# Other ticks for squares and scalings in a hybrid decoder block, all FFN quarter sums on VectorE, and the last four banks emptied by ScalarE

## The chip, the cores and the metric

The kernel runs on one core of a Trainium2 chip. The metric is the time of one execution on the device in microseconds (us); lower is better. Several engines work side by side, each through its own instructions in order, and wait for each other by semaphores: TensorE (PE, matmuls and transposes), VectorE (DVE), ScalarE (ACT), GpSimd (POOL) and SyncE (SP), whose queue issues nearly all DMA transfers. Matmul results lie in PSUM banks, which have to be read by VectorE or ScalarE before PE may write them anew.

## The reference

One decoder block over 1024 tokens of width 1024, in float32. What matters here, cut from the reference:

```python
h = rms_norm(x, g_pre_mix)
z = h @ w_in                                  # q, k, v of 24 heads, GLU input, two gates
q, k, v, glu_in, z_ga, z_gc = jnp.split(z, ...)
y_attn = dilated_attention_mixer(q, k, v, ...)
y_conv = conformer_conv_mixer(glu_in, ...)    # u * sigmoid(gate), causal conv, layer norm, silu
merged = sigmoid(z_ga) * y_attn + sigmoid(z_gc) * y_conv
x = x + rms_norm(merged @ w_mix_out, g_post_mix)
h = rms_norm(x, g_pre_ffn)
gate, up = jnp.split(h @ w_ffn_in, 2, axis=-1)
x = x + rms_norm((silu(gate) * up) @ w_ffn_out, g_post_ffn)
```

## The kernel before

Nearly all large products run as float16 matmuls of 128x512. Each operand is split into a high part (a cast, or a scaled copy, on ScalarE) and a low part (the remainder, on VectorE or POOL), and three matmuls make one product: high by high, high by low, low by high. Such a group of three is a *tick*, the unit in which the program plans: `B.later(n, step)` writes a step into the program n ticks later, and `tick()`, called behind each group of three, emits the steps that are due and moves the background generators on (`yield n` in one lets n ticks pass). There is no other scheduler. The order of each engine's instructions is the order in which the steps are emitted, and each engine waits at its next instruction until its inputs and its buffer are there.

Products that come in twos (two 128-column weight blocks against both halves of the tokens: the GLU with its gate, the second gate, q and k, and the FFN's two inputs) run as a *Winograd pair*, `winograd`: seven products in place of eight, A11, A12, S2, S1, S3, S4, A22, four ticks each, 28 ticks in all, in two banks X and Z (then V). Between them ScalarE copies a bank out: x1 after A11 (L552), x2 after S2 (L557), v1 after S1 (L562). S2 needs the first copy done, S3 the second and S4 the third, since they write on in the bank; A22 needs X read by the callback f22, which is L991 in a GLU pair and L2047 in an FFN pair. f11, f22, f12 and f21 put the results together.

For each pair the weights are prepared during the pair before. `load_ahead` issues the loads (L343 is their line), `peaks` squares them on ScalarE with a running sum (L135; the name in the trace is `junk<-d` or `junk<-b`), which bounds their size, `scales` makes powers of two of it with a small matmul on PE (L151, its input `pb` from L142), `prescale` scales whole blocks on ScalarE (L204) where the weights are used in several sums, and `quarters` makes the weight combinations: step 3 the sums for S3 and S4 (L403, L404), step 4 their split (L376, or L367 where the scale goes along; the low part is L377 on POOL or L368 on VectorE), step 5 that of A22. `pair` plans these by ticks: prescale at PRE and PRE + 1, step 4 at tick 8.

On the other side stand the token combinations: T1, T2 and then T3, T4 by `quarter_sums`, a generator, from the normed tokens. `split` makes cast (L1448) and low part (L1449).

The stages, in order: norm of x; plain GLU products and the first Winograd pair of the GLU (from about 115 us); the GLU, gate, and q/k pairs (to about 550 us); v and attention; the mix-out product (L1843) tile by tile of 128 tokens, each tile followed by `mix_norm`: residual, norm (L1563, L1565 on ScalarE), and for the fourth tile of each half, `tt == 3` and `tt == 7`, 8 groups of four transposes (L1573) into two banks with the tag "s", each emptied by ScalarE (L1579) and split. Before a tile is normed, all earlier norms but the last are run to their end (`B.finish`). Then the FFN: two plain steps (`ffn_half`, L526 the last line of their matmuls), 20 Winograd pairs, and the output product (L2170) as a Winograd product of the whole, seven products of 11 steps by four banks.

In the FFN pairs the results of two pairs are put into sums and written out to memory (`sums`, `spill`, L1899: names dqA11, dqS3 and so on), and the squares of these results (`measure`, L1872) and of the output weights (`w_square`, L1877, load L1876, name w_fo) are taken for a common scale. The loads of w_fo stand in SP's queue behind the writes of the pair before.

In the output product (`splits` is its operand work: L367 on ScalarE, L368 on VectorE, a row of 11 steps at a time) the four banks X are added at the end of product 5 into the rows `C[1]` (L2200 on VectorE), and product 6 goes on in the same banks. `right1` then squares (L2105) and scales (L2148) these rows.

Of the kernel before, what the change touches and what calls it, by code (L numbers as in the profile page):

```python
# [21 lines left out]
H = 512  # L22
# [15 lines left out]

PC = (18, 20, 26)

LF, PK, SC, PRE = 14, 22, 2, 5

TINY, W_TOP, H_TOP, A_TOP = 2.0 ** -60, 2.0 ** -13, 256.0, 2.0 ** -13

# [8 lines left out]
PLAIN = 2  # L53
# [18 lines left out]
class Build:  # L72
# [48 lines left out]

        self.nc.vector.tensor_scalar(dst.bitcast(I32), src.bitcast(I32), 0x7F800000, None, op0=OP.bitwise_and)

    def peaks(self, i):

        nc = self.nc
        m = self.tiny(2, "pk", 4)
        kind = self.jobs[i][2]
        raws = [self.raw[i - 1], self.raw[i]] if kind in ("row2", "second") else [self.raw[i]]
        for c, r in enumerate(raws):  # L130
            q = self.junk
# [3 lines left out]
            nc.scalar.activation(q, r, AF.Square, scale=W_TOP, accum_out=m[:, c:c + 1])  # L135
        q = None
        self.peak[i] = self.total(m, len(raws))

    def total(self, m, n):
        p = self.tiny(1, "pb", 4, BF16)  # L140
# [314 lines left out]
        self.flush(i)  # L455
        return self.hl.pop(i)

    def ready(self, jobs, load, peaks, scales, parts):

        i = jobs[-1]  # L460
        if load is not None:
            self.later(load, lambda: self.load_ahead(i))
        if i not in self.f16:
            self.later(parts[0], lambda: self.queue_split(i))
            return
        self.planned.update(jobs)
        if i not in self.early:
            self.later(peaks, lambda: self.peaks(i))
# [19 lines left out]
    def pair(self, i):  # L488


        J = self.jobs
        self.load_ahead(i)
        self.queue_split(i)
        self.flush(i)
        n, t = i + 1, self.ticks
        todo = [(1, lambda: self.quarters(i, 3)), (8, lambda: self.quarters(i, 4)), (10, lambda: self.quarters(i, 5))]
        if n < len(J) and J[n][2] == "row1":
            if n + 2 < len(J) and J[n + 2][2] == "row1":
                todo += [(LF, lambda: self.load_ahead(n + 3)), (PK, lambda: self.peaks(n + 3))]
# [12 lines left out]
        return self.hl[i]  # L512
# [64 lines left out]
            rest()  # L577
        f21(X)

    def quarter_sums(self, B, blocks, dt=F32R, by=None):  # L580
# [6 lines left out]
        def keep(name, x, by=None):  # L587
            x = self.split(x, H, dt, None, by)
            T[name].append((x[:, :H], x[:, H:]))


        for i in range(4):
            b11, b12, b22 = B[0][i], B[1][i], B[1][i + 4]
            t1 = self.half()
            nc.vector.tensor_tensor(t1, b11, b12, op=OP.subtract)
            nc.vector.scalar_tensor_tensor(b11, t1, -1.0, b22, op0=OP.mult, op1=OP.subtract)
            keep("T1", t1)
            yield 1
            keep("T2", b11)
            yield 3  # L600
        self.T = T
        for i in range(4):
            b11, b12, b21, b22 = B[0][i], B[1][i], B[0][i + 4], B[1][i + 4]
            if by:
                by.tensor_tensor(b22, b22, b12, op=OP.subtract)
                nc.vector.scalar_tensor_tensor(b21, b11, -1.0, b21, op0=OP.mult, op1=OP.subtract)
                yield 1
                keep("T4", b21)
                yield 0
                keep("T3", b22, by)  # L610
                yield 0
                continue
            self.wsplit.tensor_tensor(b22, b22, b12, op=OP.subtract)
            nc.vector.scalar_tensor_tensor(b21, b11, -1.0, b21, op0=OP.mult, op1=OP.subtract)
            yield 0
            keep("T3", b22)
            yield 1
            keep("T4", b21)
            yield 0
# [819 lines left out]
        x, self.spare = self.spare, None  # L1439
        return x  # L1440

    def split(self, src, n, dt=F32R, w=None, by=None):
# [5 lines left out]
        nc.scalar.copy(s[:, :n], src)  # L1448
        (by or nc.vector).tensor_tensor(s[:, 512:512 + n], src, f(s[:, :n]), op=OP.subtract)  # L1449
        return s  # L1450

    def rhs(self, ops):
# [102 lines left out]
    def mix_norm(self, tt, banks, x):  # L1555
# [9 lines left out]
        nc.scalar.activation(hn, x2, AF.Copy, scale=r)  # L1565
        self.hn[tt // 4].append(hn)
        if tt % 4 == 3:
            yield 8
            op, y = [], None
            for kt in range(8):  # L1570
                ps = self.bank("s")
                for i in range(4):
                    nc.tensor.transpose(ps[:, i * 128:(i + 1) * 128], self.hn[tt // 4][i][:, kt * 128:(kt + 1) * 128], self.ident)  # L1573
# [5 lines left out]
                nc.scalar.activation(y, ps, AF.Copy, scale=self.gain[1][:, kt:kt + 1])  # L1579
# [12 lines left out]
def build(ctx, tc, aps):  # L1592
# [81 lines left out]
    conv = B.conv()  # L1674
    next(conv)
    i = glu_pairs[0]
    B.ready((i - 1, i), 2, 14, 24, (26, 27, 31, 34, 40))
    B.later(22, lambda: B.load_ahead(i + 2))
    B.later(37, lambda: B.peaks(i + 2))
    for j in range(3, FIRST):  # L1680
# [190 lines left out]
    def measure(n, x):  # L1871
        nc.scalar.activation(B.junk[:, :H], x, AF.Square, scale=W_TOP, accum_out=sq[:, n:n + 1])  # L1872

    def w_square(n):
        x = B.slot()
        nc.sync.dma_start(x, aps["w_fo"][n])  # L1876
        B.later(14, lambda: nc.scalar.activation(B.junk, x, AF.Square, scale=W_TOP, accum_out=sw[:, n:n + 1]))  # L1877

    def power_of(dst, inv, cols):
        nc.vector.tensor_reduce(dst, cols, AX.X, OP.max)  # L1880
# [40 lines left out]
    def ffn_half(j, hf, W):  # L1921
        o = B.half()
        ps = B.unit(W[0], B.rhs(B.h2[hf]), KT)
        nc.scalar.activation(o, ps, AF.Silu, scale=B.scale[fi[j][0]][1])
        ps = B.unit(W[1], B.rhs(B.h2[hf]), KT)
        nc.vector.scalar_tensor_tensor(o, ps, B.scale[fi[j][1]][1], o, op0=OP.mult, op1=OP.mult)
        held[j, hf] = o

    B.wsplit = nc.vector
    Ws, i = [], fi[PLAIN][1]  # L1930
    B.ready((i - 1, i), 1, 12, 22, (24, 26, 30))
    B.later(46, lambda: B.load_ahead(i + 2))
# [15 lines left out]
    for j in range(0, PLAIN, 2):  # L1948
# [12 lines left out]
        x = None  # L1961

        for n in range(3):
            B.later(30 + 5 * n + j, lambda n=n, f=plain_sums: f(n))
# [71 lines left out]
    for j in range(PLAIN, FT):  # L2036
# [39 lines left out]
        if j > PLAIN:  # L2076
            for c, x in enumerate(done):
                B.later(1 + c, lambda c=c, x=x, n=2 * j - 1: measure(n + c, x))
            done = x = None
            for c in range(1 + (j < 8)):  # L2080
                if w_sent < FT:
                    B.later(1 + 4 * c, lambda n=w_sent: w_square(n))
                    w_sent += 1
        if j == FT - 2:
            assert w_sent == FT
# [35 lines left out]
            yield gap  # L2121
        C[h][t] = X2[h * 4 + t] = None

    X2, bg = {}, []

    def x2_load(i):
        X2[i] = B.slot()
# [32 lines left out]
    for i in range(7):  # L2160
# [35 lines left out]
        elif i == 5:  # L2196
            for t in range(4):
                x2_load(4 + t)
                c = C[1][t][:, R]
                nc.vector.tensor_tensor(c, X[t], c, op=OP.add)  # L2200
            bg.append(B.bg(right1()))

    for t in range(4):
# [83 lines left out]
```

## Time and profile before

| what | us |
|---|---|
| runs of the kernel: median, lowest, highest | 1616.94, 1616.76, 1619.1 |
| the profiled execution, whole | 1617.35 |
| its span in the trace | 1615.5 |
| PE busy in it | 1584.3 |
| VectorE, ScalarE, POOL busy | 1255.6, 1061.6, 460.5 |

PE's clock is granted in full (0.999 on average). In the lists of waits each row names who waited (engine, tile, line), for whom, the total in us, how often, and the longest. A timeline row gives start, duration, engine, line, operation, output and input names without their numbers, shapes, and in brackets the idle time just before it and who ended it. Rows of the windows give start and end, length, and for each engine busy time and count of instructions. `d` and `b` are weight or token blocks in SBUF, `c` half-width blocks, `p` PSUM banks.

### The profile page before, as it was taken

The page shows a single profiled execution, that of the slowest core. Times are in us where ns is not written, and L with a number is a line of the kernel's source. Part 1 is how long each engine was busy: PE and PEld are TensorE (multiplying, and loading weights), DVE is VectorE, ACT ScalarE, POOL GpSimd, SP SyncE. Part 2 cuts the span into 40 slices and gives each one's busy share as a digit, 9 for nine tenths or more (in the row PEclk, how much of TensorE's full clock was granted, in tenths as well). Part 3 has the DMA queues.
Part 4 walks back from the last instruction along what each step waited for, and adds up shares of the span by engine and source line. Part 5 has one row for each costly group of instructions (what it writes and reads, how often), then busy time and mean ns, then how long its engine had stood idle before and what let it go on. Part 6 is the DMA issues. An engine that isn't in the chain of part 4 may idle for free.

```text
span 1615.5 us, 25559 instructions
## 1 busy us (share of the span) xinstructions
PE 1584.3 (98%) x9052; PEld 897.6 (56%) x9052; DVE 1255.6 (78%) x2426; ACT 1061.6 (66%) x2024; POOL 460.5 (29%) x380
## 2 busy tenths in 40 slices
PE   8999999999999999999999999899999999999997
PEld 6744444444444799976657876444444444444443
DVE  6889999988899768787686655866666666777887
ACT  6476666778786568877752566667666666465654
POOL 0006777767777343654401200200000000000000
PEclk9999999999999999999999999999999999999999
DMA  4353333456665765677847432054344333494424
GB/s 175 109 201 112 112 131 144 146 181 206 198 179 134 234 189 159 173 226 226 249 156 274 179 118 91 27 182 163 138 144 157 124 124 137 148 382 135 156 92 163
DMA packets 162075, 265.56 MB, mean 164 GB/s; under 512 B 63665, under 2 KB 82796, under 8 KB 161948
## 3 DMA queue, kind: packets, MB, share of 16 engines
q1 hardware_dynamic: 157740, 251.77, 47.0%
q0 software_dynamic: 3920, 11.91, 2.3%
q8 instruction: 71, 1.16, 0.3%
q14 instruction: 56, 0.46, 0.1%
q10 hardware_dynamic: 288, 0.27, 0.0%
HBM read 190.05 MB, written 78.55 MB: 166 GB/s over the span
## 4 chain that ended last, share of the span: by engine, by line
PE 77%; DVE 11%; ACT 5%; issue 3%; POOL 2%; DMA 2%; SPq 0%; DVEq 0%; ACTq 0%; POOLq 0%
PE p L538 12%; PE p L540 12%; PE p L539 12%; PE p L2170 10%; PE p L522 4%; PE p L526 4%; PE p L524 4%; PE p L1843 3%; PE p L1188 2%; PE p L1190 2%; PE p L1192 2%; DVE p L931 2%; PE p L785 2%; PE p L1320 2%; PE p L1283 2%
## 5 line engine op out<-in xcount | busy, mean ns | idle before, releaser
L538 PE MATMUL p<-b,b 128*128 128x512 f16 x1032 | 390.9, 379 | 5.8 <-ACT c L552 3.6
L540 PE MATMUL p<-b,b 128*128 128x512 f16 x1032 | 391.1, 379 | 1.5 <-POOL b L377 1.5
L539 PE MATMUL p<-b,b 128*128 128x512 f16 x1032 | 391.0, 379 | 0.0
L2170 PE MATMUL p<-b 128*128 128x512 f16 x924 | 199.8, 379 | 1.1 <-DVE b L2200 1.1
L540 PEld LDWEIGHTS <-b 128*128 128x128 f16 x1032 | 100.9, 98 | 125.2 <-POOL b L377 4.0
L539 PEld LDWEIGHTS <-b 128*128 128x128 f16 x1032 | 100.8, 98 | 123.1 <-issue 7.5
L538 PEld LDWEIGHTS <-b 128*128 128x128 f16 x1032 | 100.9, 98 | 121.0
L931 DVE SCALAR_TENSOR_TENSOR p<-b,par,p 128x511 f32<-128x511 f32 (+14 forms) x232 | 163.9, 738 | 0.0
L2170 PEld LDWEIGHTS <-b 128*128 128x128 f16 x924 | 90.3, 98 | 110.3 <-issue 1.5
L522 PE MATMUL p<-b,b 128*128 128x512 f16 (+1 forms) x368 | 141.3, 384 | 1.6 <-ACT b L367 1.6
L526 PE MATMUL p<-b,b 128*128 128x512 f16 (+1 forms) x368 | 140.7, 382 | 0.4 <-DVE b L368 0.4
L524 PE MATMUL p<-b,b 128*128 128x512 f16 (+1 forms) x368 | 140.6, 382 | 0.0
L368 DVE SCALAR_TENSOR_TENSOR b<-d,sc,b 128x1024 f16<-128x1024 f32 x40 | 51.3, 1281 | 86.1 <-ACT b L367 86.1
L377 POOL TENSOR_TENSOR b<-d,b 128x1024 f16<-128x1024 f32 x44 | 93.9, 2135 | 83.7 <-ACT b L376 83.7
L1190 PE MATMUL p<-b,b 128*128 128x256 f16 x384 | 104.7, 273 | 0.0
L1192 PE MATMUL p<-b,b 128*128 128x256 f16 x384 | 104.7, 273 | 0.0
L1188 PE MATMUL p<-b,b 128*128 128x256 f16 x384 | 104.7, 273 | 0.0
L1843 PE MATMUL p<-b,b 128*128 128x512 f32 x384 | 90.0, 392 | 0.0
L1297 ACT ACTIVATE c<-c,stat 128x128 f32<-128x128 f32 (+1 forms) x192 | 84.4, 444 | 6.8 <-DVE stat L1287 6.7
L931 DVE SCALAR_TENSOR_TENSOR p<-c,pairs,p 128x511 f32<-128x511 f32 (+6 forms) x112 | 82.6, 738 | 0.0
L1287 DVE CUSTOM_DVE_ANT_0 c<-p,bt,sig 128x128 f32<-128x128 f32 (+1 forms) x192 | 70.7, 406 | 14.8 <-PE p L1283 11.8
L1843 PEld LDWEIGHTS p<-b,b 128*128 128x128 f32 x384 | 71.3, 188 | 14.3
(329 smaller groups left out, 3485.4 us busy)
## 6 DMA issues: line engine op xcount, KB each, us to landing
b<-w_in SPq DMA_DIRECT2D x30, 512.0 KB, 6.1
b<-w_v SPq DMA_DIRECT2D x24, 512.0 KB, 4.5
b<-w_fi SPq DMA_DIRECT2D x24, 512.0 KB, 6.9
d<-w_in SPq DMA_DIRECT2D x23, 512.0 KB, 4.0
dqS<-c SPq DMA_DIRECT2D x44, 256.0 KB, 2.0
b<-w_fo SPq DMA_DIRECT2D x22, 512.0 KB, 4.0
b<-w_fo SPq DMA_DIRECT2D x44, 256.0 KB, 5.4
c<-dqS SPq DMA_DIRECT2D x44, 256.0 KB, 4.2
```

What stands on the lines that cost most here:

```text
L522: nc.tensor.matmul(ps, hi[:, s], a, start=kt == 0, stop=False)
L524: nc.tensor.matmul(ps, hi[:, s], b, start=False, stop=False)
L526: nc.tensor.matmul(ps, lo[:, s], a, start=False, stop=kt == nk - 1)
L538: nc.tensor.matmul(ps, hi[:, s], a, start=first and kt == 0, stop=False, skip_group_check=True)
L539: nc.tensor.matmul(ps, hi[:, s], b, start=False, stop=False, skip_group_check=True)
L540: nc.tensor.matmul(ps, lo[:, s], a, start=False, stop=kt == 3, skip_group_check=True)
L931: nc.vector.scalar_tensor_tensor(A[i][:, j:], src[i][:, :H - j], w[i], A[i][:, j:], op0=OP.mult, op1=OP.add)
L1188: nc.tensor.matmul(o, a, hi[:, s], start=kt == 0, stop=False)
L1190: nc.tensor.matmul(o, a, lo[:, s], start=False, stop=False)
L1192: nc.tensor.matmul(o, b, hi[:, s], start=False, stop=kt == KT - 1)
L1843: nc.tensor.matmul(banks[tt][nh], st, wt[:, nh * H:(nh + 1) * H], start=bool(kt == 0 and a), stop=bool(kt == KT - 1 and b))
L2170: nc.tensor.matmul(acc[t], x, y, start=first and e == 0, stop=last and e == 2, skip_group_check=True)
```

## The change

1. The first GLU pair (`ready` with the new argument `apart`): the squares of its two weight blocks are taken apart, at ticks 11 and 17 in place of both at 14; its two scalings and three quarters at 30, 33, 35, 36, 41 in place of 26, 27, 31, 34, 40.
2. All pairs with scaling: `PRE` from 5 to 8, and the split for S3 and S4 from tick 8 to 7, so that it comes ahead of the next pair's scalings.
3. FFN quarter sums: the path on POOL is gone; VectorE makes all sums and low parts, T3 before T4.
4. The squares of the plain FFN results are taken in `ffn_half`, two or three ticks after the result; before, within the first pair at ticks 10, 11, 12 and 15. The maxima of the second pair's weights move from tick 58 to 65.
5. The transposes of the first half of the tokens start 14 ticks after their last tile's norm in place of 8.
6. The squares of w_fo start with pair `j = 4` in place of 3; pairs 4 to 9 have two, the others one. Both loads are issued at the pair's start, the squares stand at ticks 15 and 11; before, the loads were planned at ticks 1 and 5 and the squares 14 ticks behind them.
7. At the end of the output product's sixth part, ScalarE copies the four banks X into `xc`, and `right1` adds from there, row by row.

```diff
-LF, PK, SC, PRE = 14, 22, 2, 5
+LF, PK, SC, PRE = 14, 22, 2, 8
...
+    def peaks(self, i, apart=0, first=None):
...
+            if c == 0 and apart and len(raws) > 1:
+                self.later(apart, lambda: self.peaks(i, 0, m))
+                return
...
-        todo = [(1, lambda: self.quarters(i, 3)), (8, lambda: self.quarters(i, 4)), (10, lambda: self.quarters(i, 5))]
+        todo = [(1, lambda: self.quarters(i, 3)), (7 if n + 1 in self.pre else 8, lambda: self.quarters(i, 4)), (10, lambda: self.quarters(i, 5))]
...
-            if by:
-                by.tensor_tensor(b22, b22, b12, op=OP.subtract)
-                nc.vector.scalar_tensor_tensor(b21, b11, -1.0, b21, op0=OP.mult, op1=OP.subtract)
-                yield 1
-                keep("T4", b21)
-                yield 0
-                keep("T3", b22, by)
-                yield 0
-                continue
             self.wsplit.tensor_tensor(b22, b22, b12, op=OP.subtract)
             nc.vector.scalar_tensor_tensor(b21, b11, -1.0, b21, op0=OP.mult, op1=OP.subtract)
             yield 0
...
-            yield 8
+            yield 14 if tt == 3 else 8
...
-    B.ready((i - 1, i), 2, 14, 24, (26, 27, 31, 34, 40))
+    B.ready((i - 1, i), 2, 11, 24, (30, 33, 35, 36, 41), 6)
...
-    def w_square(n):
+    def w_square(n, at):
         x = B.slot()
         nc.sync.dma_start(x, aps["w_fo"][n])
-        B.later(14, lambda: nc.scalar.activation(B.junk, x, AF.Square, scale=W_TOP, accum_out=sw[:, n:n + 1]))
+        B.later(at, lambda: nc.scalar.activation(B.junk, x, AF.Square, scale=W_TOP, accum_out=sw[:, n:n + 1]))
...
+        B.later(3 - j * hf, lambda: measure(2 * j + hf + 1, o))
...
-    B.later(58, lambda: B.peaks(i + 2))
+    B.later(65, lambda: B.peaks(i + 2))
...
-    qs = B.bg(B.quarter_sums(B.h2f, (h2[0][:4], h2[0][4:], h2[1][4:]), F16, nc.gpsimd))
+    qs = B.bg(B.quarter_sums(B.h2f, (h2[0][:4], h2[0][4:], h2[1][4:]), F16))
...
-        for n, x in enumerate([held[j + e, hf] for e in range(2) for hf in range(2)]):
-            B.later((10, 11, 12, 15)[n], lambda n=2 * j + n + 1, x=x: measure(n, x))
...
-            for c in range(1 + (j < 8)):
+        if j > PLAIN + 1:
+            for c in range(1 + (j < 10)):
                 if w_sent < FT:
-                    B.later(1 + 4 * c, lambda n=w_sent: w_square(n))
+                    w_square(w_sent, 15 - 4 * c)
                     w_sent += 1
...
     def right1():
         for t in range(4):
             c = C[1][t][:, R]
+            nc.vector.tensor_tensor(c, xc[t], c, op=OP.add)
+            xc[t] = None
...
         elif i == 5:
             for t in range(4):
                 x2_load(4 + t)
-                c = C[1][t][:, R]
-                nc.vector.tensor_tensor(c, X[t], c, op=OP.add)
+            xc = [B.half() for _ in range(4)]
+            snap(xc, X)
             bg.append(B.bg(right1()))
```

Three places show what this does to the order of instructions. Lines of the changed file are a few off: L557, L562 and L567 there are the bank copies L552, L557 and L562, and L372, L2038, L1873 are L367, L2044, L1877.

ScalarE in an FFN pair (`j = 6`), from the copy of x1 to the next pair's split, before:

```order
L552 COPY c_12508<-p_12506 128x512
L367 ACTIVATE b_12552<-b_12514,sc_12372 128x1024
L367 ACTIVATE c_12562<-b_12285,sc_12372 128x512
L557 COPY c_12509<-p_12506 128x512
L2044 ACTIVATE c_12508<-c_12508,sc_12372 128x512
L1877 ACTIVATE junk,sw<-b_12518 128x1024
L562 COPY c_12510<-p_12572 128x512
L367 ACTIVATE b_12598<-d_12429,sc_12523 128x1024
```

and now:

```order
L557 COPY c_12506<-p_12504 128x512
L372 ACTIVATE b_12546<-b_12512,sc_12368 128x1024
L372 ACTIVATE c_12556<-b_12280,sc_12368 128x512
L1873 ACTIVATE junk,sw<-b_12502 128x1024
L562 COPY c_12507<-p_12504 128x512
L2038 ACTIVATE c_12506<-c_12506,sc_12368 128x512
L1873 ACTIVATE junk,sw<-b_12500 128x1024
L567 COPY c_12508<-p_12567 128x512
L372 ACTIVATE b_12593<-d_12424,sc_12519 128x1024
```

A square stands ahead of the copy of x2 and another ahead of that of v1; b_12502 is the second of the pair's two loads. Before, one stood ahead of the copy of v1 and the other behind the split.

PE at the end of the transposes of the first half, before:

```order
L1573 MATMUL p_11281<-ident,b_11131 128x128
L1843 MATMUL p_11164<-b_10788,b_10626 128x512
L1843 MATMUL p_11165<-b_10788,b_10626 128x512
L1843 MATMUL p_11164<-b_10789,b_10626 128x512
L1843 MATMUL p_11165<-b_10789,b_10626 128x512
L1843 MATMUL p_11164<-b_10788,b_10626 128x512
L1843 MATMUL p_11165<-b_10788,b_10626 128x512
L1573 MATMUL p_11298<-ident,b_10942 128x128
```

and now:

```order
L1839 MATMUL p_11164<-b_10814,b_10670 128x512
L1839 MATMUL p_11165<-b_10814,b_10670 128x512
L1569 MATMUL p_11289<-ident,b_10942 128x128
L1569 MATMUL p_11289<-ident,b_10953 128x128
L1569 MATMUL p_11289<-ident,b_11049 128x128
L1569 MATMUL p_11289<-ident,b_11131 128x128
L1569 MATMUL p_11302<-ident,b_10942 128x128
L1569 MATMUL p_11302<-ident,b_10953 128x128
L1569 MATMUL p_11302<-ident,b_11049 128x128
L1569 MATMUL p_11302<-ident,b_11131 128x128
L1569 MATMUL p_11311<-ident,b_10942 128x128
```

Each `p` is one group's bank. Before, six matmuls of a tile (L1843) stood between any two groups; now the fifth to the eighth group follow each other, since the next tile's norm runs this one to its end.

VectorE behind the sixth part of the output product, before:

```order
L2200 TENSOR_TENSOR b_15866<-p_14892,b_15866 128x512
L2200 TENSOR_TENSOR b_15867<-p_14893,b_15867 128x512
L2200 TENSOR_TENSOR b_15868<-p_14894,b_15868 128x512
L2200 TENSOR_TENSOR b_15869<-p_14895,b_15869 128x512
L2148 TENSOR_TENSOR b_15866<-b_15866,b_14874 128x512
L2149 TENSOR_SCALAR so_14888<-so_14888 128x1
L368 SCALAR_TENSOR_TENSOR b_16389<-c_16326,fs,b_16389 128x512
```

and now:

```order
L2142 TENSOR_TENSOR b_15866<-c_16376,b_15866 128x512
L2145 TENSOR_TENSOR b_15866<-b_15866,b_14874 128x512
L2146 TENSOR_SCALAR so_14888<-so_14888 128x1
L373 SCALAR_TENSOR_TENSOR b_16394<-c_16326,fs,b_16394 128x512
L373 SCALAR_TENSOR_TENSOR b_16394<-b_15373,fs,b_16394 128x512
L2142 TENSOR_TENSOR b_15867<-c_16377,b_15867 128x512
```

The add of a row (L2142, from ScalarE's copy) now comes right before its gain (L2145), and the split's low parts (L373) of the next step stand between one row's add and the next; before, all four adds came first.

More of the change, by code (lines that the diff above doesn't have):

```diff
@@ L122, in power @@
         self.nc.vector.tensor_scalar(dst.bitcast(I32), src.bitcast(I32), 0x7F800000, None, op0=OP.bitwise_and)
-    def peaks(self, i):
+    def peaks(self, i, apart=0, first=None):
         nc = self.nc
-        m = self.tiny(2, "pk", 4)
+        m = self.tiny(2, "pk", 4) if first is None else first
         kind = self.jobs[i][2]
@@ L130, in peaks @@
         for c, r in enumerate(raws):
+            if c == 0 and first is not None:
+                continue
             q = self.junk
@@ L135, in peaks @@
             nc.scalar.activation(q, r, AF.Square, scale=W_TOP, accum_out=m[:, c:c + 1])
+            if c == 0 and apart and len(raws) > 1:
+                self.later(apart, lambda: self.peaks(i, 0, m))
+                return
         q = None
-        self.peak[i] = self.total(m, len(raws))
+        self.peak[i] = self.total(m, 2 if first is not None else len(raws))
     def total(self, m, n):
@@ L456, in weights, with ready @@
         return self.hl.pop(i)
-    def ready(self, jobs, load, peaks, scales, parts):
+    def ready(self, jobs, load, peaks, scales, parts, apart=0):
         i = jobs[-1]
@@ L467, in ready @@
         if i not in self.early:
-            self.later(peaks, lambda: self.peaks(i))
+            self.later(peaks, lambda: self.peaks(i, apart))
             self.later(scales, lambda: self.scales(i))
@@ L578, in winograd, with quarter_sums @@
         f21(X)
-    def quarter_sums(self, B, blocks, dt=F32R, by=None):
+    def quarter_sums(self, B, blocks, dt=F32R):
         nc = self.nc
@@ L585, in quarter_sums, with keep @@
         T["B11"], T["B21"], T["B22"] = blocks
-        def keep(name, x, by=None):
-            x = self.split(x, H, dt, None, by)
+        def keep(name, x):
+            x = self.split(x, H, dt)
             T[name].append((x[:, :H], x[:, H:]))
@@ L1440, in packed, with split @@
         return x
-    def split(self, src, n, dt=F32R, w=None, by=None):
+    def split(self, src, n, dt=F32R, w=None):
         nc = self.nc
@@ L1448, in split @@
         nc.scalar.copy(s[:, :n], src)
-        (by or nc.vector).tensor_tensor(s[:, 512:512 + n], src, f(s[:, :n]), op=OP.subtract)
+        nc.vector.tensor_tensor(s[:, 512:512 + n], src, f(s[:, :n]), op=OP.subtract)
         return s
@@ L1957, in plain_sums @@
                 q.clear()
-        for n, x in enumerate([held[j + e, hf] for e in range(2) for hf in range(2)]):
-            B.later((10, 11, 12, 15)[n], lambda n=2 * j + n + 1, x=x: measure(n, x))
-        x = None
         for n in range(3):
@@ L2122, in out_norm @@
         C[h][t] = X2[h * 4 + t] = None
-    X2, bg = {}, []
+    X2, bg, xc = {}, [], None
     def x2_load(i):
```

## The prediction

> **What bounds the kernel now.** I read the page first, then the waits of TensorE, then each place where one of those waits or an edit lies, in the timeline and in the order of the instructions.
>
> ```profile
> PE 1584.3 (98%) x9052; PEld 897.6 (56%) x9052; DVE 1255.6 (78%) x2426; ACT 1061.6 (66%) x2024; POOL 460.5 (29%) x380
> ...
> PE p L538 <- ACT c L552: 3.6, 2, 3.2
> PE p L538 <- DVE c L2047: 2.4, 3, 1.5
> PE p L522 <- ACT b L367: 1.6, 2, 1.0
> PE p L540 <- POOL b L377: 1.5, 5, 0.5
> PE p L538 <- ACT c L557: 1.5, 2, 1.2
> PE p L1573 <- ACT b L1579: 1.4, 1, 1.4
> ...
> PE p L2170 <- DVE b L2200: 1.1, 1, 1.1
> ...
> PE p L538 <- DVE c L991: 0.6, 2, 0.3
> ...
> PE p L538 <- ACT c L562: 0.4, 1, 0.4
> ```
>
> TensorE (PE) is busy for 1584.3 of 1615.5 us, so all waits together hold 31 us, and only what moves a start of PE counts. The waits that the edits aim at are those listed: total us, times, longest. So I replay each edited place by hand: the new order of instructions, with the durations of the profiled execution. PE starts a matmul every 0.216 us; three are one tick, 0.65 us; a Winograd pair is 28 ticks, 18.15 us.
>
> **The FFN's w_fo squares.** This is the largest loss I find. Six pairs now hold two squares (L1877, 1.04 us) at ticks 11 and 15 of the pair, ahead of ScalarE's copies of a bank; before they stood behind them. The one at tick 11 is that of the second load. The pair that begins at 1116.3 shows the chain that this meets.
>
> ```profile
> 1120.18 0.91 SPq L1876 DMA_DIRECT2D b<-w_fo  x2
> ...
> 1124.09 0.59 ACT L557 COPY c<-p 128x512 f32<-128x512 f32 x1 [1.35 <-PE p L540]
> 1124.58 0.72 ACT L2044 ACTIVATE c<-c,sc 128x512 f32<-128x512 f32 x1
> 1125.20 1.04 ACT L1877 ACTIVATE junk<-b 128x1024 bf16<-128x1024 f32 x1
> ...
> 1126.68 0.59 ACT L562 COPY c<-p 128x512 f32<-128x512 f32 x1 [0.35 <-PE p L540]
> ...
> 1128.35 1.28 DVE L368 SCALAR_TENSOR_TENSOR b<-d,sc,b 128x1024 f16<-128x1024 f32 x1 [3.64 <-ACT b L367]
> ...
> 1130.88 0.68 DVE L2047 TENSOR_TENSOR c<-p,c 128x512 f32<-128x512 f32 x1
> ...
> 1131.66 0.38 PE L538 MATMUL p<-b,c 128*128 128x512 f16 x1
> ```
>
> The third copy (L562) is followed by the next pair's split (L367), VectorE's part of it (L368), two sums and L2047, and at 1131.66 the product A22 starts, 0.1 us after L2047 ends: the chain has no slack, so what delays L562 delays PE. The same trace holds a case of it:
>
> ```profile
> 1156.45 0.45 SPq L1876 DMA_DIRECT2D b<-w_fo  x1
> ...
> 1162.39 1.06 ACT L1877 ACTIVATE junk<-b 128x1024 bf16<-128x1024 f32 x1 [0.78 <-DMA b<-w_fo]
> ...
> 1167.76 0.38 PE L540 MATMUL p<-b,b 128*128 128x512 f16 x1
> 1168.36 0.38 PE L538 MATMUL p<-b,c 128*128 128x512 f16 x1 [0.23 <-DVE c L2047]
> ```
>
> There a load took 5.9 us from its issue, ScalarE stood still for it, and PE lost 0.39 us between starts (0.60 against the 0.216 of an unbroken stream).
>
> In every second pair five results are written out first, so the loads leave some 4 us after the pair's start, here the second at 1120.7. When it lands is bounded by two places. Below: a pair of such loads with little ahead of it,
>
> ```profile
> 1072.28 0.41 SPq L343 DMA_DIRECT2D b<-w_fi  x1
> ...
> 1077.05 1.06 ACT L135 ACTIVATE junk<-b 128x1024 bf16<-128x1024 f32 x1
> ```
>
> at most 4.8 us. Above: 5.9 us for a first load, and a second one another 0.8 later, 6.7. I take 5.5, landing at 1126.2. Then on ScalarE: square 1.06, copy L557 and scaling L2044 at 0.49 and 0.62 from start to start, second square 1.06: L562 starts at 1129.4 instead of 1126.7, and less the 0.1 of slack PE loses 2.6 us, part of it already at S3, which needs the copy L557. With 4.8 it is 1.9, with 6.7 it is 3.8. The new order has three such pairs: 7.8 us, less the 0.4 that is there already, **+7.4** (5.3 to 11.0). In the other three pairs the loads leave 1.5 us sooner and the squares fit within 0.3 us of the copies: 0.
>
> [...]
>
> **The start of the FFN.** VectorE makes GpSimd's (POOL's) eight sums and low parts, T3 before T4.
>
> ```profile
> 1019.99 1.59 DVE L1449 TENSOR_TENSOR b<-b,b 128x512 f16<-128x512 f32 x1
> ...
> 1019.48 1.56 POOL L605 TENSOR_TENSOR b<-b,b 128x512 f32<-128x512 f32 x1 [106.33 <-DVE b L596]
> ...
> 1043.71 0.38 PE L538 MATMUL p<-b,b 128*128 128x512 f16 x1 [3.24 <-ACT c L552]
> ```
>
> Eight more VectorE instructions cost 8 x 0.69 = 5.5 us; while POOL worked beside it, an instruction that elsewhere takes 0.68 took 1.59, and the six that were stretched give about 5.4 back. What is gained is the order and ScalarE's freedom: the squares and the next pair's maxima go behind the casts. Replayed, T3 is complete at 1043.2 instead of 1046.6, and S2 starts at 1041.9, S3 at 1047.1, A22 at 1052.3, the second pair at 1054.9, all without a wait. In the second pair two w_fo loads no longer stand in SP's queue ahead of the write that L1913 waits for, and the first squares are gone from ScalarE: its two waits vanish too, and the third pair starts without one. So the waits on L552, L557, L562 and L2047 go but the one at 1168.36: 3.6 + 1.2 + 0.4 + 2.2 = 7.4 us of idle time, 8.4 between starts (each restart costs 0.16 more, as at 1168.36). Two small ones come: one measure square of 0.63 between the second half's transposes delays a copy by 0.6, and the scales' matmul (L151, due at 1037.0) waits 0.9 for maxima that now come after the casts. **-6.9** (-4 to -7.5).
>
> **The transposes of the first half.** They start six ticks later, and so the last four groups of four run back to back before the next tile, in two banks.
>
> ```profile
> 963.08 1.15 ACT L1565 ACTIVATE b<-d,rr 128x1024 f32<-128x1024 f32 x1 [0.86 <-DVE rr L1533]
> ...
> 965.26 0.68 ACT L1579 ACTIVATE b<-p,hg 128x512 f32<-128x512 f32 x1
> 965.97 0.62 ACT L1448 CAST b<-b 128x512 f16<-128x512 f32 x1
> ...
> 965.99 0.66 PE L1573 MATMUL p<-ident,b 128*128 128x128 f32 x4 [1.38 <-ACT b L1579]
> ```
>
> The old wait, 1.6 between starts, goes. But a group is 0.43 us on PE and 1.25 on ScalarE (copy and cast), and the norm of tile 4 stands between the first two. Replayed, the fourth group waits 1.2, the sixth 0.7, the seventh 1.25, the eighth 0.8; the next tile starts at 970.6 instead of 968.3. **+2.3** (+1.0 to +2.7).
>
> **GLU and projection pairs.** Casts of S3 and S4 go ahead of the scalings in all of them.
>
> ```profile
> 151.00:170.00 19.00, 18.39 (x86) 8.15 (x85) 18.84 (x32) 11.99 (x19) 12.84 (x9) 1.00 0.25 85
> ...
> 431.73 1.28 POOL L404 TENSOR_TENSOR b<-d,d 128x512 f32<-128x512 f32 x1
> ...
> 437.48 0.38 PE L538 MATMUL p<-b,b 128*128 128x512 f16 x1 [0.24 <-ACT c L557]
> ```
>
> In the GLU pairs the POOL waits go, but VectorE is busy 18.84 of 19.00 us from one pair to the next, and A22 waits for its L991: what PE gains at S3 it loses there, 0. In the projection pairs POOL's sum L404 ends at 433.0; ScalarE now waits for it before the scalings (1.15 each), and the copy that S3 waits for already at 437.48 comes about 1.0 later. One more pair is like it, with less; one POOL wait (0.34 between starts) goes. **+1.0** (0 to +1.5).
>
> **The first GLU pair.** The first square moves ahead of a weight split that ran at 87.6.
>
> ```profile
> d<-w_in SPq DMA_DIRECT2D x1, 512.0 KB, 5.6
> ```
>
> The load that it squares left at 83.4 and lands at 89.0, so the split moves to 90.2, and a new wait of about 1.8 us on it stands against the two on L367 that go or shrink. **0** (-2.0 to +0.5; the gain if the load were 1.4 us faster).
>
> **The end.** ScalarE's four copies are done before PE returns to the banks, so the wait on L2200 goes: -1.2 between starts. But the adds are then spread out.
>
> ```profile
> 1578.89 2.47 DVE L2200 TENSOR_TENSOR b<-p,b 128x512 f32<-128x512 f32 x4
> ...
> 1596.46 0.74 DVE L368 SCALAR_TENSOR_TENSOR b<-b,fs,b 128x512 f16<-128x512 f32 x1
> ...
> 1597.63 0.81 PE L2170 MATMUL p<-b 128*128 128x512 f16 x3
> ```
>
> Each add now stands right before its row's gain, behind the splits, and its square on ScalarE waits for it ahead of the next split. The fourth add ends at 1590.5, its square at 1591.3, and every split behind it is 1.6 us late. The last split part ends at 1598.8 instead of 1597.2, and the matmul that reads it started at 1598.06 (the third of the last row): it is 0.8 late. **+0.8** (-1.2 to +1.2).
>
> **Sum.** -6.9 + 7.4 + 2.3 + 1.0 + 0 + 0.8 = +4.6, on the profiled execution's 1617.35 us; the median of the runs is 0.4 lower, so 1621.5. Under 0.2%, 3.2 us, a run of this kernel can hardly be told from no change.
>
> **Rivals.** The page's own medians, the last figure of the row, are the base of two of them.
>
> ```profile
> dqS<-c SPq DMA_DIRECT2D x44, 256.0 KB, 2.0
> b<-w_fo SPq DMA_DIRECT2D x22, 512.0 KB, 4.0
> ```
>
> (1) The second w_fo loads land after 4.0 us, the median. Then L562 is 1.2 late, PE loses 1.1 per pair, 2.9 in all, and the sum is +0.1: 1617.0. For it: a shorter median; against it: the 5.9 us, in just such a pair. (2) Loads land soon everywhere: 2.7 us from the issue takes the squares out of the way (results of half the size, on their way out, land in 2.0), so the w_fo term is -0.4 and the first pair's -1.9: 1611.8, faster. [...] It decides at 2.7 us, and the rows speak against it. (3) VectorE has no room for its eight more instructions at the FFN's start, and A22 of the first two pairs waits for L2047 as before: half of the 6.9 stays away, 1625. For it: in my replay L2047 of the second pair ends just when A22 is due.
>
> **Chances.** The sum as it stands 0.55, within 1618.5 to 1624.5; (1) 0.18, (2) 0.12, (3) 0.15. Of the first, a fifth lies below 1620.2. So slower 0.44 + 0.14 = 0.58, within 0.2% 0.11 + 0.18 = 0.29, faster 0.13. The range leaves out most of (2) and the worse half of (3): 1613.5 to 1626.
>
> **What would show it.** Right: PE waits at S3 and A22 in three of the six FFN pairs with two squares, the third to the eighth, behind a square that waits for w_fo; no wait above 1 us in the first two pairs, the third pair about 7 us earlier against the tile before; three waits on L1579 before tile 6; no wait on L2200, but one near the end on L368. Wrong: squares that start right at tick 11, or a first FFN pair that still waits for a copy.

## The result, and the profile after

The changed kernel takes 1623.36 us (median of 6 runs, 1621.89 to 1624.72) against 1616.85 us before (6 runs, 1616.49 to 1619.1): a ratio of 1.0037, 95% interval 1.0025 to 1.0050. It is slower by 6.5 us, 0.4%. A second series of 5 runs gave 1621.97 us (ratio 1.0033, 1.0021 to 1.0046); all 11 runs together have the median 1622.9, and differences to the changed kernel below are taken from that. The 95% interval of one kernel's time is about 1.4 us to either side with 11 runs, and about 2 us with 5 or 6.

The profiled execution took 1624.18 us with a span of 1622.4. This is the first line of its page, and its list of TensorE's waits (total us, times, longest), with the lines of the changed file:

```profile
PE 1586.5 (98%) x9052; PEld 898.5 (55%) x9052; DVE 1259.6 (78%) x2434; ACT 1063.7 (66%) x2028; POOL 449.8 (28%) x372
...
PE p L543 <- DVE c L987: 3.7, 3, 2.3
PE p L1569 <- ACT b L1575: 3.6, 5, 1.2
PE p L543 <- DVE c L2041: 3.2, 3, 1.1
PE p L543 <- DVE c L1027: 2.0, 1, 2.0
PE p L543 <- ACT c L562: 2.0, 3, 1.3
PE p L527 <- ACT b L372: 1.7, 1, 1.7
PE p L2167 <- DVE b L373: 1.5, 3, 0.5
...
PE p L156 <- ACT pb L147: 0.6, 1, 0.6
```

The waits on POOL (1.5), on L552 (3.6) and on L2200 (1.1) of before are gone. In their place stand A22 in the GLU pairs (L987, and L1027 in the pair behind them: 5.7), A22 behind the squares of w_fo (L2041: 3.2), the transposes (L1575: 3.6, before 1.4) and the end (L373: 1.5). PE's busy time is 2.2 us longer with the same number of matmuls: part of them ran at half rate, one every 0.427 us in place of 0.216 (below).

The table sets each term of the prediction beside the lost time between PE's starts (the excess of every start over the 0.216 us of an unbroken stream, summed over the stretch), in us, each column from one profiled execution. The start's first load took another 0.4.

| term | before | after | measured | forecast |
|---|---|---|---|---|
| start of the FFN, first pairs | 8.4 | 1.1 | -7.3 | -6.9 |
| squares of w_fo | 0.4 | 4.5 | +4.1 | +7.4 |
| transposes of the first half | 1.6 | 3.6 | +2.1 | +2.3 |
| projection pairs | 2.1 | 3.4 | +1.3 | +1.0 |
| GLU pairs | 3.4 | 8.0 | +4.6 | 0 |
| first GLU pair | 3.5 | 3.8 | +0.3 | 0 |
| the end | 1.2 | 2.0 | +0.8 | +0.8 |
| sum | | | +5.9 | +4.6 |

So the FFN's start brought what it promised, and two places decide the rest, which the forecast had wrong in opposite directions: the GLU pairs and the w_fo squares.

### The profile page after: what moved, and what is told of

Same layout as the page of the kernel before. It is cut to its first block, busy times and chain, and to the rows that moved or that the text cites. A ratio compares the mean times of both kernels' runs of the same rounds, so it can differ in the third digit from the quotient of the medians.

```text
span 1622.4 us, 25551 instructions
## 1 busy us (share of the span) xinstructions
PE 1586.5 (98%) x9052; PEld 898.5 (55%) x9052; DVE 1259.6 (78%) x2434; ACT 1063.7 (66%) x2028; POOL 449.8 (28%) x372
## 4 chain that ended last, share of the span: by engine, by line
PE 73%; DVE 13%; ACT 6%; issue 3%; DMA 2%; POOL 2%; SPq 0%; DVEq 0%; ACTq 0%; POOLq 0%
PE p L543 11%; PE p L544 11%; PE p L545 11%; PE p L2167 9%; PE p L527 4%; PE p L531 4%; PE p L529 4%; DVE p L927 3%; PE p L1839 3%; PE p L1184 2%; PE p L1188 2%; PE p L1186 2%; PE p L781 2%; DVE b L373 2%; PE p L1316 2%
## 5 line engine op out<-in xcount | busy, mean ns | idle before, releaser
L373 DVE SCALAR_TENSOR_TENSOR b<-d,sc,b 128x1024 f16<-128x1024 f32 x40 | 51.2, 1281 | 89.9 <-ACT b L372 89.9
```

## Experiments

Every kernel is named by what stands in it; differences are against the changed kernel (1622.9) where nothing else is said.

**1. The GLU pairs: where do 4.6 us come from?** First the rows. VectorE (DVE) and POOL in the second GLU pair after the change, and PE where A22 waits; then the same VectorE instruction before, and the POOL instruction in question there:

```profile
156.96 2.14 POOL L382 TENSOR_TENSOR b<-b,b 128x1024 f16<-128x1024 f32 x1 [1.16 <-ACT b L381]
...
157.28 0.15 DVE L159 TENSOR_SCALAR sc<-sc 128x1 f32<-128x1 f32 x1
...
157.55 1.57 DVE L186 TENSOR_SCALAR sc<-hs,sc 128x3 f32<-128x3 f32 x1
159.03 0.73 DVE L927 SCALAR_TENSOR_TENSOR p<-b,par,p 128x502 f32<-128x502 f32 x1
...
169.45 0.38 PE L543 MATMUL p<-b,c 128*128 128x512 f16 x1 [2.31 <-DVE c L987]
```

```profile
156.74 0.21 DVE L181 TENSOR_SCALAR sc<-hs,sc 128x3 f32<-128x3 f32 x1
156.86 0.74 DVE L931 SCALAR_TENSOR_TENSOR p<-b,par,p 128x502 f32<-128x502 f32 x1
...
160.06 2.14 POOL L377 TENSOR_TENSOR b<-b,b 128x1024 f16<-128x1024 f32 x1 [5.07 <-ACT b L376]
```

L186 multiplies 128x3 numbers. Before, it took 0.21 us, and POOL's low part of S3 and S4 began three us behind it. Now the cast stands ahead of the scalings, POOL begins at 156.96, and L186 takes 1.57 us: it ends at 159.12, when POOL's instruction ends (159.10). In the third pair, where it happens to stand in a gap of POOL's, it takes 0.21; in the fourth, beside POOL again, 1.74:

```profile
176.16 1.72 POOL L409 TENSOR_TENSOR b<-d,d 128x512 f32<-128x512 f32 x1
...
177.96 0.21 DVE L186 TENSOR_SCALAR sc<-hs,sc 128x3 f32<-128x3 f32 x1
...
179.04 2.14 POOL L382 TENSOR_TENSOR b<-b,b 128x1024 f16<-128x1024 f32 x1 [1.16 <-ACT b L381]
...
196.53 2.13 POOL L382 TENSOR_TENSOR b<-b,b 128x1024 f16<-128x1024 f32 x1 [1.16 <-ACT b L381]
...
196.95 1.74 DVE L186 TENSOR_SCALAR sc<-hs,sc 128x3 f32<-128x3 f32 x1
```

The end of L186 lies 0.02 us behind that of POOL's instruction here and 0.03 in the fourth pair; the 128x1 product L159 (0.15 us), in the same stretch beside the same instruction, was not held, and no run here shows what sets the two apart.

Two kernels test whether POOL's instruction holds L186. One puts the order of the GLU and projection pairs back:

```diff
-LF, PK, SC, PRE = 14, 22, 2, 8
+LF, PK, SC, PRE = 14, 22, 2, 5
...
-        todo = [..., (7 if n + 1 in self.pre else 8, lambda: self.quarters(i, 4)), ...]
+        todo = [..., (8, lambda: self.quarters(i, 4)), ...]
```

> The changed kernel with PRE 5 and the split for S3 and S4 at tick 8, as before the change. Theory (the tick order in the GLU pairs makes POOL's low part overlap a small VectorE instruction, and VectorE has no slack): the waits of A22 fall back from 6.3 us to 1.4, the half-rate matmuls go, the POOL waits of 2.0 come back, and the projection pairs give 1.3 back; 1623.4 - 4.4 - 1.3 = 1617.7 us. Rival (the GLU waits have another source, and only the projection pairs answer to this edit): 1622.1 us.

Measured: 1619.36 us (11 runs), 3.5 less. In its profile the GLU pairs lose 4.5 us in place of 8.0 and the projection pairs 2.1 in place of 3.4. The waits of A22 are down to 0.6 idle and those on POOL are back (1.8), with one on a bank copy (L562, 0.5). The time falls between theory and rival. The other leaves the order alone and takes L186 off VectorE, in the pairs of the later stages up to 508.7 us too (21 products):

```diff
-        nc.vector.tensor_scalar(u, self.unscale[i >= self.fi0], a, None, op0=OP.mult)
+        self.later(9, lambda: nc.scalar.activation(u, self.unscale[0], AF.Copy, scale=a)) if self.conv_sums else nc.vector.tensor_scalar(u, self.unscale[i >= self.fi0], a, None, op0=OP.mult)
```

> The changed kernel, but in the GLU pairs the 128x3 scale product (L186) is made by ScalarE nine ticks later, where ScalarE has room, in place of VectorE. Everything else stays, the early POOL low part too. Theory (L186 is held until POOL's low part ends, 1.57 and 1.74 us in place of 0.21, and A22 pays for it): the waits of A22 at about 169 and 209 us lose 1.4 and 1.5 us, and the half-rate stretch behind the second goes (1.5): 1623.4 - 4.4 = 1619.0 us. Rival (VectorE is simply full; the time shows up in whichever VectorE instruction stands beside POOL's): under 0.5 us, 1623.

Measured: 1619.93 us (11 runs), 3.0 less. Its rows at the same place, of ScalarE and PE, and its waits from 112 to 232 us:

```profile
160.44 0.30 ACT L186 ACTIVATE sc<-hs,sc 128x3 f32<-128x3 f32 x1
...
168.18 0.38 PE L543 MATMUL p<-b,c 128*128 128x512 f16 x1 [0.98 <-DVE c L987]
...
PE p L543 <- DVE c L987: 2.1, 3, 1.0
PE p L543 <- DVE c L1027: 0.4, 1, 0.4
```

POOL's low part is as early as in the changed kernel, yet the idle time in front of A22 falls from 2.31 to 0.98 at this place and from 2.0 to 0.4 at the fourth pair, and the GLU pairs lose 3.1 us in all, less than the 3.4 before the change. So it is this one instruction, held for POOL, and not VectorE's load as such: the rival is out. That the time gained only 3.0 and not 4.4 has its rows elsewhere in the same execution: a half-rate stretch in the first GLU pair (1.7) and 6.1 us in the w_fo pairs in place of 4.5. Against that the projection pairs, which the edit reaches too, lost 2.3 in place of 3.4.

**2. What a wait costs beside itself.** The fourth pair of the changed kernel, PE's rows, and the granted clock (after the busy times: PEclk, share of DMA, GB/s):

```profile
209.02 0.38 PE L543 MATMUL p<-b,c 128*128 128x512 f16 x1 [1.98 <-DVE c L1027]
...
210.00 0.63 PE L544 MATMUL p<-b,c 128*128 128x512 f16 x1
210.43 0.63 PE L545 MATMUL p<-b,c 128*128 128x512 f16 x1
...
212.99 0.46 PE L545 MATMUL p<-b,c 128*128 128x512 f16 x1
213.29 0.38 PE L543 MATMUL p<-b,b 128*128 128x512 f16 x1
...
210.20:213.30 3.10, 3.10 (x10) 1.04 (x8) 3.10 (x6) 1.18 (x2) 2.56 (x2) 0.52 0.28 109
```

One us after the wait, matmuls start every 0.427 us in place of 0.216 for 3.3 us: another 1.7 us lost. The trace's record of the clock has 0.5 for 3.41 us there. The changed kernel was run again to see whether that belongs to it.

> The changed kernel once more, beside the others of this call and in more runs. Expected 1623.4 us, between 1621.9 and 1624.7. Theory (what is lost in the GLU and w_fo pairs depends on where POOL's low part, the landing of a load and the clock happen to fall): another profile shows other waits at the same places, in sum 5 to 8 us from 112 to 232 us and 4 to 6 us in the w_fo pairs. Rival (the waits are the same in each execution): 8.0 and 4.5 us again.

Measured: 1621.97 us (5 runs, 1621.16 to 1623.98). The same wait, to 0.04 us, without the slow stretch:

```profile
208.49 0.38 PE L543 MATMUL p<-b,c 128*128 128x512 f16 x1 [1.94 <-DVE c L1027]
...
210.42 0.38 PE L543 MATMUL p<-b,c 128*128 128x512 f16 x1
...
208.00:212.00 4.00, 3.52 (x17) 1.62 (x17) 4.00 (x7) 2.66 (x4) 2.77 (x2) 1.00 0.17 66
```

Its GLU pairs lose 6.3 us, its w_fo pairs 4.2: within the theory's bounds, but the waits in the GLU pairs are the same to 0.04 us, as the rival had it, and what differs is the clock behind them. In the profiles of the other kernels with this GLU order the slow stretch stands behind the fourth pair's wait (twice), the second's (twice), or the wait in the first GLU pair (twice), and once behind the four waits at the transposes. In both executions in which it came behind the second pair's wait, VectorE caught up during it: the third pair's wait was gone, the fourth pair's was 0.3 in place of 2.1, and these GLU pairs lost 5.2 and 5.3 us, less than the 6.3 without a slow stretch. The w_fo pairs lost 4.0 to 6.1 in the executions with these squares. How much of the spread of 2.3 to 4.6 us in the runs of these kernels comes from either is not shown: the kernel before, in whose profile no such stretch follows a wait, spreads by 2.9 us over 27 runs. What decides whether a stretch follows a wait is not shown either: of the waits of 1.98 and 1.94 us at the same place one was followed by it and one was not, and the 3.24 us of idle time before the change (at 1043.71) were followed by none.

**3. The squares of w_fo.** The third FFN pair after the change: the issue of both loads, ScalarE, and PE at A22.

```profile
1085.44 0.91 SPq L1872 DMA_DIRECT2D b<-w_fo  x2
...
1090.76 1.06 ACT L1873 ACTIVATE junk<-b 128x1024 bf16<-128x1024 f32 x1 [2.76 <-DMA b<-w_fo]
1091.82 0.57 ACT L562 COPY c<-p 128x512 f32<-128x512 f32 x1
...
1092.90 1.04 ACT L1873 ACTIVATE junk<-b 128x1024 bf16<-128x1024 f32 x1
1093.94 0.57 ACT L567 COPY c<-p 128x512 f32<-128x512 f32 x1
...
1098.86 0.38 PE L543 MATMUL p<-b,c 128*128 128x512 f16 x1 [1.09 <-DVE c L2041]
```

ScalarE stands still for 2.76 us for the second load, and both copies wait behind it. One kernel changes a single number, so that the first load's square is the first:

```diff
-                    w_square(w_sent, 15 - 4 * c)
+                    w_square(w_sent, 11 + 4 * c)
```

> The changed kernel with one number changed: the square at tick 11 is that of the first of the pair's two loads, the one at tick 15 that of the second. Theory (the loss is the landing of the second load, which comes 1.3 to 1.8 us after the first, ahead of the copy of x2): both squares are over 1.3 us earlier, L562 and L567 too, and the 4.5 us in the w_fo pairs fall under 1: 1619.5 us. Rival (any square ahead of these copies costs it): above 1622.5.

Measured: 1619.15 us (11 runs), 3.7 less. The same place:

```profile
1088.65 1.06 ACT L1873 ACTIVATE junk<-b 128x1024 bf16<-128x1024 f32 x1 [1.28 <-DMA b<-w_fo]
1089.70 0.57 ACT L562 COPY c<-p 128x512 f32<-128x512 f32 x1
...
1090.79 1.04 ACT L1873 ACTIVATE junk<-b 128x1024 bf16<-128x1024 f32 x1
1091.83 0.57 ACT L567 COPY c<-p 128x512 f32<-128x512 f32 x1
```

The first square starts 4.3 us after the pair's L557 (1084.37 in this run), where it was 5.8 (1085.00), so L562 and L567 come 1.5 earlier against that copy, and of 4.5 us in the w_fo pairs 0.6 remains. The loss is the second load, not a square ahead of a copy as such. The other kernel puts the squares behind the copies, as before the change:

```diff
-    def w_square(n, at):
+    def w_square(n):
...
-        B.later(at, lambda: nc.scalar.activation(B.junk, x, ...
+        B.later(14, lambda: nc.scalar.activation(B.junk, x, ...
...
-                    w_square(w_sent, 15 - 4 * c)
+                    B.later(1 + 4 * c, lambda n=w_sent: w_square(n))
```

> The changed kernel with the w_fo loads at ticks 1 and 5 and the squares 14 ticks behind them, behind the copies of x2 and v1, as before the change; pairs and counts stay as changed (pairs 4 to 9 have two). Theory (what the trace of after shows at S3 and A22): the waits of 4.4 us in the third, fifth and seventh pair go, 0.4 may come back: 1619.2 us. Rival (the term is as large as forecast, 7.4, part of it not visible as waits): 1616.0 us.

Measured: 1617.18 us (11 runs), 5.7 less; the ratio to before is 0.9999 (0.9990 to 1.0008). Its profile has no wait left in the w_fo pairs, so 4.5 us of the gain are these. The other 1.2 lie within the interval; in the profiled execution the GLU pairs, whose code is the same, lost 5.2 in place of 8.0. The runs do not settle between 4.5 and 5.7.

**4. The FFN's start alone.** The kernel before with only parts 3, 4 and the later start of the w_fo squares (their loads and squares in the old places).

> The kernel before with only the FFN's start changed: quarter sums on VectorE, the plain results' squares two or three ticks behind them, maxima at tick 65, and the w_fo squares from pair 4 on but in their old place behind the copies. Theory (all of the 7.3 us at the FFN's start is the gain of this part, and it needs nothing else): 1616.9 - 7.3 = 1609.6 us. Rival (VectorE has no room without the other edits, A22 waits for L2041): 1613.

Measured: 1609.80 us (5 runs, 1609.52 to 1610.24), ratio 0.9953 (0.9940 to 0.9965): 7.0 us faster than before. From 1012 to 1300 us PE has one wait on another engine:

```profile
PE p L156 <- ACT pb L147: 0.7, 1, 0.7
```

Which of the edits does it? One kernel gives T3's sums back to POOL, T4 first (the POOL path in `quarter_sums` is back as before):

```diff
...
-    qs = B.bg(B.quarter_sums(B.h2f, (h2[0][:4], h2[0][4:], h2[1][4:]), F16))
+    qs = B.bg(B.quarter_sums(B.h2f, (h2[0][:4], h2[0][4:], h2[1][4:]), F16, nc.gpsimd))
```

> The kernel ffn_alone (1609.8 us), but the eight sums and low parts of T3 are on POOL again and T4 comes ahead of T3; the squares and maxima keep their new places. Theory (the long wait at the FFN's start is the casts that wait for POOL's sums, ahead of the copy that S3 needs; the squares cost the second wait only): 3.4 us of wait on L557 come back in the first pair, with up to 0.8 at A22: 1613.5 us. Rival (the moved squares and maxima are what freed the start): 1610.5 or less.

Another gives the squares and maxima their old ticks back:

```diff
-        B.later(3 - j * hf, lambda: measure(2 * j + hf + 1, o))
...
-    B.later(65, lambda: B.peaks(i + 2))
+    B.later(58, lambda: B.peaks(i + 2))
...
+        for n, x in enumerate([held[j + e, hf] for e in range(2) for hf in range(2)]):
+            B.later((10, 11, 12, 15)[n], lambda n=2 * j + n + 1, x=x: measure(n, x))
```

> The kernel ffn_alone (1609.8 us), but the plain results' squares are at ticks 10, 11, 12 and 15 of the first pair again and the maxima at tick 58; VectorE keeps all sums. Theory (the squares stand ahead of the copies L562 and L567 and were the second wait, 1.4 us, and part of the second pair's 2.3): 1.5 to 3 us come back, 1612 us. Rival (with VectorE's sums the casts are early enough to hide the squares): 1610.

Measured: 1611.49 us with POOL's sums (5 runs, 1611.01 to 1613.38), 1612.51 us with the old squares (6 runs, 1612.03 to 1613.14). PE's waits at the FFN's start, first with POOL's sums, then with the old squares:

```profile
1039.58 0.16 PE L156 MATMUL p<-pb,ones 128*128 128x1 bf16 x1 [2.10 <-ACT pb L147]
```

```profile
1042.64 0.38 PE L543 MATMUL p<-b,b 128*128 128x512 f16 x1 [1.55 <-ACT c L557]
1049.17 0.38 PE L543 MATMUL p<-b,b 128*128 128x512 f16 x1 [1.19 <-ACT c L562]
1055.17 0.38 PE L543 MATMUL p<-b,c 128*128 128x512 f16 x1 [0.66 <-DVE c L2043]
```

The expectation for POOL's sums fell: the wait on L557 does not come back. The casts still stand still for POOL, but the maxima now come behind them, and PE meets the delay at the scales' matmul, 2.1 us in place of 0.7. In this execution, the slowest of the five, a half-rate stretch that cost 1.6 us followed that wait. For the old squares the theory held, 2.7 us. Without the one edit 1.7 us of the 7.0 are lost, without the other 2.7. The waits from 1060 us on (3.2 between starts before) are gone in all three kernels; what all three share is the w_fo squares' later start, which points to it, but it was not run alone.

**5. Transposes and end.** One kernel has the old tick for the transposes:

```diff
-            yield 14 if tt == 3 else 8
+            yield 8
```

> The changed kernel with the transposes of the first half eight ticks behind the norm, as before the change. Theory (the trace of after: 3.6 us at L1575 against 1.6): 1623.4 - 2.1 = 1621.3 us. Rival (the later start of the next tile is made good in the mix-out stage): 1623.4.

Measured: 1620.65 us (11 runs), 2.3 less, where the theory had 2.1. PE's groups after the change, each with its wait:

```profile
970.96 0.66 PE L1569 MATMUL p<-ident,b 128*128 128x128 f32 x4 [1.19 <-ACT b L1575]
972.84 0.60 PE L1569 MATMUL p<-ident,b 128*128 128x128 f32 x4
973.90 0.66 PE L1569 MATMUL p<-ident,b 128*128 128x128 f32 x4 [0.46 <-ACT b L1575]
975.61 0.66 PE L1569 MATMUL p<-ident,b 128*128 128x128 f32 x4 [1.05 <-ACT b L1575]
976.85 0.65 PE L1569 MATMUL p<-ident,b 128*128 128x128 f32 x4 [0.58 <-ACT b L1575]
```

With the old tick only the first is left (1.40 at 970.01). At the end, the other keeps ScalarE's copies and adds all four rows at once:

```diff
             snap(xc, X)
+            for t in range(4):
+                c = C[1][t][:, R]
+                nc.vector.tensor_tensor(c, xc[t], c, op=OP.add)
...
-            nc.vector.tensor_tensor(c, xc[t], c, op=OP.add)
```

> The changed kernel with ScalarE's four copies kept, but the four adds together ahead of the first row's square and gain. Theory (the spread of the adds makes the splits late, the copies do not): no wait on the bank and no wait on L373 at the end, 1623.4 - 2.0 = 1621.4 us. Rival (ScalarE's four copies alone make the splits late): the waits of 0.65 stay, 1623.

Measured: 1620.26 us (11 runs, 1618.71 to 1623.28), 2.6 less with an interval of about 1.4 to either side. The last waits of PE, first after the change, then here:

```profile
1602.27 0.81 PE L2167 MATMUL p<-b 128*128 128x512 f16 x3 [0.49 <-DVE b L373]
1603.60 0.81 PE L2167 MATMUL p<-b 128*128 128x512 f16 x3 [0.52 <-DVE b L373]
1604.92 1.24 PE L2167 MATMUL p<-b 128*128 128x512 f16 x5 [0.52 <-DVE b L373]
```

```profile
1604.03 2.32 PE L2165 MATMUL p<-b 128*128 128x512 f16 x10 [0.28 <-DVE b L373]
```

From 2.0 us between starts to 0.4. The same code varies here: the end loses 1.9 to 2.5 us in the seven profiles with the spread adds, and 0.4, 0.0 and 1.0 in the three with the adds together (this one and the two kernels of part 6), where the kernel before lost 1.2. So it was the spread of the adds that made the splits late; that the copies never do is not shown.

**6. A version that beats both.** The FFN's start alone with this end:

> The kernel ffn_alone (1609.8 us) with ScalarE's four copies at the end of the sixth part and the four adds together behind them. Expected: 1.24 us of wait at the end become 0.44: 1609.0 us, faster than before by 7.9 us. Rival (the four copies cost the splits elsewhere): 1609.8 or more.

Measured: 1609.44 us (5 runs), ratio to before 0.9951 (0.9939 to 0.9964): 7.5 to 7.7 us faster than before and 13.5 faster than the changed kernel. In its profile the wait on the bank is gone; against the FFN's start alone (1609.80) the time is not told apart, so it stays open between the 1609.0 expected and the rival. A last one moves the scales one tick for the wait that is left:

```diff
-    B.ready((i - 1, i), 1, 12, 22, (24, 26, 30))
+    B.ready((i - 1, i), 1, 12, 23, (24, 26, 30))
```

> The kernel best with the scales of the first FFN pair one tick later (23 in place of 22), since L156 there waits 0.8 us for maxima that now come behind the casts. Expected if that wait is all: 0.65 less than best, 1608.3 us. Rival (the quarters behind it become late and the first pair waits): no gain, 1609 or more.

Measured: 1609.61 us (5 runs), no gain. In its profile L156 still loses 1.1 us between starts, 0.8 without the edit: the rival's outcome, though not by its way, since no copy of the first pair waits.

## Why the prediction was right or wrong

The direction and the range were right (slower, 1613.5 to 1626); the time was 1.9 us low. That it came so close is luck: two larger errors had opposite signs.

- *Start of the FFN*, -6.9: right. In the trace -7.3, alone on the chip -7.0. The matmul of the scales (0.8, forecast 0.9) and one group of transposes (0.3, forecast 0.6) waited as the replay had it. Rival (3), VectorE without room, did not happen: no wait on L2041 in the first two pairs.
- *Squares of w_fo*, +7.4: the mechanism was right, in the three pairs named (third, fifth, seventh), but mis-sized: +4.1. The failed step is "I take 5.5, landing at 1126.2". In the rows above the second load was issued at 1085.9 and squared from 1090.76, 4.8 us later; in the other two pairs 4.7 and 5.4 passed. That takes 0.1 to 0.8 off each pair. The loads also left earlier against PE: the second one 4.2, 3.9 and 3.8 us after its pair's first matmul, where it was 4.6 in the pair that was replayed (which began at 1116.1). That takes off another 0.4 to 0.8, and of 2.6 per pair 1.5, 1.1 and 1.7 are left; 1.6, 1.2 and 1.7 were measured. The chain from L567 to A22 took 4.9 us in all three, 5.0 before. Rivals (1) and (2), landing after 4.0 and 2.7 us, are out.
- *GLU pairs*, 0: wrong, +4.6, of which 1.7 are the half-rate stretch. The failed step is "what PE gains at S3 it loses there". The exchange as such held: with L186 off VectorE the pairs lose 3.1 us against 3.4 before, the 2.0 at POOL's waits gone and those of A22 grown from 1.4 to 3.1. But the step did not ask which VectorE instructions the earlier POOL instruction would now meet: L186, held twice, is the other 2.9. What would have told stood in the trace before: the shortest, median and longest ns of that instruction there,

```profile
L181 DVE TENSOR_SCALAR sc<-hs,sc x22: 209/844/1753, 118.7 to 502.6; 128x3 f32<-128x3 f32 x22
```

It took 0.21 us in the first five pairs and up to 1.75 in later ones, where no wait of PE on VectorE followed. Fifteen of the 22 took over 0.3 us, and each of these ended 0.02 to 0.03 us behind an instruction of POOL.
- *Transposes* +2.3 (measured 2.1), *projection pairs* +1.0 (1.3), *first GLU pair* 0 (0.3), *end* +0.8 (0.8): right, each at the wait named, the end's in three waits and not one. The new wait on the split of the first GLU pair was 1.7 us, forecast 1.8.

## What to carry to other kernels

Before moving an instruction on one engine, look which instructions of a full engine it will now run beside, the tiniest too: a product of 128x3, held twice for over 1.5 us, cost 2.9 us. A square that waits for a load belongs behind the copies that free the banks, and of two loads the first one's work goes first: one number was worth 3.7 us. Behind the same wait of PE of two us, one execution lost 1.7 more at a granted clock of 0.5 and the next nothing, so differences of that size need many runs or the waits themselves.

## What the runs showed of the hardware

A VectorE product of 128x3 float32 in SBUF took 1.57 and 1.74 us beside POOL's 2.14 us instruction and 0.21 in a gap of POOL's, while 128x1 instructions in the same stretch took 0.15 to 0.16. Behind the kernel's start the 14 profiles have 18 waits of PE with 1.6 us or more of idle time; 8 of them (1.8 to 2.3 us) were followed by 3.4 us at a granted clock of 0.5, about eight matmuls at 0.427 us, and 10 were not, among them the longest (3.24). The second load of 512 KB behind the writes of two pairs took 4.7 to 5.4 us here from its issue to the square that waited for it.
